# Constants packed so that the operands of the matrix products start at other offsets in a partition

## The chip, the cores and the metric

The kernel runs on one core of one Trainium2 chip. The metric is device time in microseconds (us), the median of three runs: 1645.25 us before the change (1645.24 to 1646.19). The engines are named as the profile names them: PE multiplies matrices (PEld is its loading of weights), DVE and ACT work elementwise, POOL is almost unused here, and SP issues nearly all transfers. SBUF, the memory on the core, has 128 partitions; a tile takes the same bytes of every partition, so its place is one number, its **offset** in a partition. This text is about those offsets.

## The reference, cut to what matters

A two-layer encoder over 512 tokens of 1024 features, all in float32. Each layer normalises, projects to 6144 columns, runs differential attention and a two-way gated recurrence (HGRN2) side by side, merges them under gates, and adds a SwiGLU feed-forward network of 2816 hidden features:

```python
for layer in range(DEPTH):
    h = rmsnorm(x, attn_norm[layer])
    proj = h @ w_in[layer]
    ...
    y_a = diff_attention(a_q, a_k, a_v, ...) @ w_a[layer]
    y_b = hgrn2_bidirectional(b_q, b_ff, b_fb, b_i, b_g, ...) @ w_b[layer]
    merged = jax.nn.sigmoid(gate_a) * y_a + jax.nn.sigmoid(gate_b) * y_b
    x = x + merged @ w_o[layer]
    h = rmsnorm(x, ffn_norm[layer])
    x = x + (jax.nn.silu(h @ w_gate[layer]) * (h @ w_up[layer])) @ w_down[layer]
return rmsnorm(x, final_norm)
```

## The kernel before

**Products in three parts.** Each float32 operand of a large product is split into a high part (rounded to the type that the code calls F32R) and a low part, the rest. `mm3` (L209 to L211) then issues three matmuls into one sum: high by high, high by low, low by high. One matmul has a *stationary* operand, 128x128, which PE loads first, and a *moving* one, 128 partitions by 512 columns of 4 bytes, which is 2048 bytes of each partition. In the profile `m<-hh,hi` is: output `m`, moving operand `hh`, stationary operand `hi`.

**Who moves and who stands.** `xT` is the residual, `hh` and `hl` are the two parts of the normed input: 8 chunks of 128 features by 512 tokens, so 2048 bytes a chunk. The weights come in by `wload` into two buffers `raw`, and `wsplit` makes `hi` (ACT, L92) and `lo` (DVE, L81) of them, three buffers each. `project_fm` and the feed-forward loop hold the weights still and move the activations (`hh`, `hl`, `mh`, `ml`, `obh`, `obl`, `oah`, `oal`, or `gh`, `gl`). `project_tm` and the last `w_down` hold the activations still (512 bytes of a chunk at a time) and move the weights.

**Stages of a layer.** Projections from `hh`, `hl` and the HGRN2 heads, four projections with tokens on partitions (`project_tm`), attention, `w_b` and `w_a`, `w_o` (moving `mh`, `ml`), then gate and up of the feed-forward network (moving `hh`, `hl`), then `w_down` (`gh`, `gl`: moving in the first layer, stationary in the second). Of the matmuls with 512 moving columns, 3648 move `hh` or `hl`, 768 have `hh` or `hl` stationary, and 2120 have neither.

**What sets the order.** A scheduler orders each engine's instructions by the order of the code, by priority (`urgent`) and by some orders written by hand (`behind`). It doesn't look at offsets.

**What sets the offsets.** Pools take SBUF in the order in which they are opened, and a tile takes its size rounded up to 32 bytes. The pool `const` comes first, behind 1152 bytes that the system keeps. In it `eps` and `one`, 4 bytes each, take 32 bytes each, and `rcol` and `rcol8`, 16 bytes each, stand behind `hh`, `hl` and `rbc`. Behind `const` come `wraw` (`raw`), `wsplit` (`hi`, `lo`), `small`, and then the pools that each stage opens.

Of the kernel before, what the change touches and what calls it, by code (L numbers as in the profile page):

```python
# [9 lines left out]
F32 = mybir.dt.float32  # L10
# [8 lines left out]
P = 128  # L19
# [12 lines left out]

# column offsets of the combined input projection
A_Q, A_K, A_V, B_Q, B_FF, B_FB, B_I, B_G, G_A, G_B = (
    0, 512, 1024, 1536, 2048, 2560, 3072, 3584, 4096, 5120)

# columns of the transposed small vectors
V_ATT, V_FFN, V_DA, V_HG, V_LB = 0, 16, 32, 40, 48


def _bits(x, n):
    """x cut to n significand bits."""
    m, e = math.frexp(x)
    return math.ldexp(math.floor(m * (1 << n)), e - n)
# [3 lines left out]
def kernel(  # L48
# [45 lines left out]
    def behind(ins, other):  # L94
        """Queue ins after other, on whatever engines they are."""
        tc.add_manual_dep(ins.ins, other.ins.name,
                          mybir.DependencyInfo(mybir.DependencyClass.NoSync, mybir.DependencyReason.DATA),
                          reason="keep the tensor engine from waiting")
# [13 lines left out]

    # ---------------------------------------------------------------- constants
    ident = cp.tile([P, P], F32, name="ident")
# [4 lines left out]
    DVE.tensor_copy(ones_r, ones)  # L119
    eps = cp.tile([P, 1], F32, name="eps")  # L120
    DVE.memset(eps, EPS)
    one = cp.tile([P, 1], F32, name="one")
    DVE.memset(one, 1.0)
# [3 lines left out]

    # block-diagonal masks of blocks of 2**j tokens, j = 0..4
    masks = cp.tile([P, 5, P], I8, name="masks")
# [8 lines left out]

    # ------------------------------------------------- residual and normed input
    xT = cp.tile([P, DC, T], F32, name="xT")  # L140
    hh = cp.tile([P, DC, T], F32R, tag="hh", name="hh")
    hl = cp.tile([P, DC, T], F32R, tag="hl", name="hl")
    rbc = cp.tile([P, T], F32, name="rbc")
    rcol = cp.tile([P, TC], F32, name="rcol")
    rcol8 = cp.tile([P, TC], F32, name="rcol8")
    sacc = cp.tile([P, T], F32, name="sacc")
# [3 lines left out]
    def normed(src, c, gain):  # L150
        """Chunk c of the normed input, up to the row scale, in two parts."""
        hi = act(hh[:, c, :], src, AF.Copy, scale=gain)
        return hi, stt(hl[:, c, :], src, gain, hh[:, c, :].bitcast(F32), ALU.mult, ALU.subtract)
# [9 lines left out]
    def absorb(c, gain, first):  # L163
        """Chunk c of the new residual."""
        normed(xT[:, c, :], c, gain)
        squares(c, first)
# [20 lines left out]

    # ------------------------------------------------------------ weight streams
    def wload(src):
        """src: [p, k, c] of DRAM."""  # L190
        _, k, c = src.shape
        raw = wp.tile([P, 2048], F32, tag="raw", name="raw")
        v = raw[:, :k * c].rearrange("p (k c) -> p k c", c=c)
        load(v, src)
        return v

    def wsplit(v):
        """hi and lo parts of v [p, k, c]."""
        _, k, c = v.shape
        hi = hp.tile([P, 1024], F32R, tag="hi", name="hi")[:, :k * c].rearrange("p (k c) -> p k c", c=c)  # L200
        lo = hp.tile([P, 1024], F32R, tag="lo", name="lo")[:, :k * c].rearrange("p (k c) -> p k c", c=c)
        split_act(v, hi, lo)
        return hi, lo
# [9 lines left out]
    def project_fm(w, cols, evac, k=DC, ah=None, al=None):  # L213
        """Output features on partitions; cols: list of first columns (128 wide), pairs adjacent."""
        ah = hh if ah is None else ah
# [21 lines left out]
    def project_tm(w, c0, evac):  # L237
        """512 output features from column c0, tokens on partitions."""
        ps = [mbank() for _ in range(TC)]
# [15 lines left out]

    # ------------------------------------------------------------------- start
    lnexp = ACT.preload_act_table_set("natural_log_exp_and_others")
# [8 lines left out]
    with tc.tile_pool(name="init", bufs=1, reuse_waits="tile") as ip:  # L266
# [41 lines left out]
        with tc.issue_after(norms[-1][1].ins):  # L308
            for c in range(DC):
                squares(c, c == 0)  # L310

            # differential weights [1, -lambda] of each layer
            lv = lam.rearrange("p (g j e) -> p g j e", j=2, e=64)
# [12 lines left out]

            # lower bounds of the second layer's forget gates, columns (direction, head)
            lg = vecs[:, V_LB:V_LB + 16].rearrange("p (d l h) -> p d l h", d=2, l=2)
# [17 lines left out]

            # rotary tables
            sins = []
# [36 lines left out]

    # ------------------------------------------------------------------- HGRN2
    def sigmoid(v):
        """In place, by exponentials and logarithms alone."""
        act(v, v, AF.Exp, scale=-1.0)
        act(v, v, AF.Ln, bias=one)  # L390
        return act(v, v, AF.Exp, scale=-1.0)
# [10 lines left out]
    def head_norm(ps, sq, sh, sl, gain, mark):  # L402
        """rmsnorm of ps [value, token] over its partitions, times gain."""
        ss = bank("hss")
        mm = PE.matmul(ss, ones_r, sh, start=True, stop=False)
        if mark is not None:
            behind(mm, mark)
        PE.matmul(ss, ones_r, sl, start=False, stop=True)
        rsqrt_mean(sq, ss, P)
        stt(sq, ps, gain, sq, ALU.mult, ALU.mult)  # L410
        return sq

    def hgrn_head(l, h, q, z, sg, vB, oh, ol, hgp):
        """q [P,T]; z [P,2,T] gate inputs (forward, backward); sg [P,T] output gate input;
        vB [P,TC,512]; oh, ol [P,T] result in two parts."""
        flat = lambda v: v.rearrange("p d c -> p (d c)")
        blocks = lambda v: v.rearrange("p (b c) -> p b c", c=64)
        # log forget gates g, with a zero before each 64 tokens, and log keys lk
        lk = hgp.tile([P, 2, T], F32, tag="lk", name="lk")
# [10 lines left out]
        else:  # L430
# [9 lines left out]
            tt(lk, lk, z, ALU.subtract)  # L440
        # products of each query with its own token's key and, times one decay, its neighbour's
        kk = z
# [7 lines left out]
        tt(kk, kk, q.unsqueeze(1).to_broadcast([P, 2, T]), ALU.mult)  # L450
        # sums within 64 tokens: cf, cb inclusive, xb exclusive; key exponents
        for d in range(2):
# [5 lines left out]
        tt(ab, ab, xb, ALU.add)  # L458
        # totals of 64 tokens; before and from each 64 within its chunk of 128; decays of whole chunks
        tot = cum[:, :, :, 64]  # L460
# [10 lines left out]
        def chunk_states(d):  # L471
            """Queries decayed from (to) the chunk's edge and the states they meet there."""
            f = hgp.tile([P, 2, T], F32, tag="fac", name="fs", bufs=FAC)
# [17 lines left out]
        def turned(f, kc):  # L491
            """The keys with their tokens on partitions."""
            pt = bank("kt")
# [23 lines left out]
        def level(L):  # L517
            """Decayed queries and keys of the blocks of 2 L tokens about their middles."""
            f = hgp.tile([P, 2, T], F32, tag="fac", name="fl", bufs=FAC)
# [22 lines left out]

        # transposed scores within chunks: rows s, columns t
        A = hgp.tile([P, TC, P], F32, tag="A", name="A")
# [9 lines left out]
        def place(L, pv):  # L554
            """The blocks of 2 L tokens of A."""
            if L == 64:
# [12 lines left out]
        kb, turn = turned(fb, bk)  # L569
        # the wide levels first; each narrower one takes its blocks over  # L570
        done = None
# [39 lines left out]

    # --------------------------------------------------------------- attention
    def rope(v, tp):
        """v [P, TC, 512], in place."""
        w = v.rearrange("p t (g e) -> p t g e", e=64)
# [11 lines left out]

    def attention(l, aq, ak, avh, avl, oh, ol, ap):
        """aq, ak (rotated, queries scaled) [P, TC, 512]; avh, avl the values in two parts;
        oh, ol [P, HEADS, T] result in two parts."""  # L630

        def operands(h):
            """Each component's two parts stacked on the partitions: queries, keys, keys the other way round."""
            half = [slice(0, 64), slice(64, 128)]
# [20 lines left out]
        def exps(q2, ka, kb, t, mark):  # L655
            """Exponentials of both components' scores of 128 queries, and their sums."""
            tok = slice(t * P, (t + 1) * P)
# [61 lines left out]

    # ------------------------------------------------------------------ layers  # L720
    last_silu = None
    for l in range(LAYERS):
        win = w_in[l]
        an = [vecs[:, V_FFN + 8 * l + c:V_FFN + 8 * l + c + 1] for c in range(DC)]
        with ExitStack() as mix:
# [10 lines left out]
            def scaled(dst):  # L736
                """dst(i): where tile i goes."""
                return lambda i, ps: tt(dst(i), ps, rbc, ALU.mult)
# [180 lines left out]
def _layout(inputs):  # L919
    """The input with its features first; the vectors that go with features as columns of 128."""  # L920
    import numpy as _np
# [27 lines left out]
```

## Time and profile before

| | |
|---|---|
| median of the runs | 1645.25 us |
| the profiled execution, first to last instruction | 1645.1 us |
| instructions | 18701 |
| DVE busy | 1011.9 us (62%) |
| ACT busy | 777.0 us (47%) |
| bytes moved | 142.53 MB, mean 87 GB/s |

The span of the profiled execution is 0.15 us under the median, so nearly nothing lies around it. Matmuls overlap one another: the profile gives one with 512 columns some 390 to 400 ns, but the next starts after some 230 ns. What a matmul costs in a dense row is therefore the distance from its start to the next start. It is read from the timeline, or from the number of matmuls in a stretch.

### The profile page before, as it was taken

How to read it: one execution, taken by the hardware profiler on the slowest of the kernel's cores; microseconds unless marked ns; L12 is line 12 of the kernel's file. 1: busy time of each engine (PE TensorE's matmuls, PEld its weight loads, DVE VectorE, ACT ScalarE, POOL GpSimd, SP SyncE). 2: the span in 40 equal slices, each digit the busy share in tenths (PEclk: the TensorE clock that was granted, in tenths of full speed). 3: DMA queues.
4: the chain of work that ended last, by engine and by line, in shares of the span. 5: the costliest groups of instructions: out<-in, count | busy, mean ns of one | idle time of the engine just before them, and what ended most of it. 6: DMA issues, size and time to landing. Idle time of an engine off the chain costs nothing.

```text
span 1645.1 us, 18701 instructions
## 1 busy us (share of the span) xinstructions
PE 1625.3 (99%) x7456; PEld 1325.9 (81%) x7456; DVE 1011.9 (62%) x1626; ACT 777.0 (47%) x1192; POOL 7.8 (0%) x21
## 2 busy tenths in 40 slices
PE   8999999999999999999999999999999999999998
PEld 6788888887888888888878888888878888888886
DVE  7878977877644444433368789688875444444224
ACT  5666666676432322322255567676744323224213
POOL 1000000000000000000000000000000000000000
PEclk9999999999999999999999999999999999999999
DMA  5312212221332223322232222122123233322321
GB/s 186 96 58 77 77 52 77 77 77 51 103 102 85 92 79 102 103 90 97 97 101 77 77 77 75 56 76 77 51 78 103 77 103 103 103 94 98 103 79 75
DMA packets 118823, 142.53 MB, mean 87 GB/s; under 512 B 3024, under 2 KB 101328, under 8 KB 118736
## 3 DMA queue, kind: packets, MB, share of 16 engines
q1 hardware_dynamic: 118592, 141.31, 26.1%
q8 instruction: 58, 0.95, 0.2%
q14 instruction: 29, 0.24, 0.0%
q10 hardware_dynamic: 144, 0.03, 0.0%
HBM read 139.23 MB, written 2.10 MB: 86 GB/s over the span
## 4 chain that ended last, share of the span: by engine, by line
PE 94%; DVE 3%; ACT 2%; issue 1%; DMA 0%; SPq 0%; ACTq 0%
PE m L211 27%; PE m L209 27%; PE m L210 27%; PE sc L550 2%; DVE fl L81 1%; PE po L600 1%; PE s L209 1%; PE s L210 1%; PE s L211 1%; PE qk L666 1%; PE wt L713 1%; PE qk L663 1%; PE st L503 1%; ACT fl L78 0%; DVE lo L81 0%
## 5 line engine op out<-in xcount | busy, mean ns | idle before, releaser
L92 ACT CAST hi<-raw 128x1024 fp32r<-128x1024 f32 (+2 forms) x280 | 276.5, 989 | 631.3 <-PE m L210 486.6
L209 PE MATMUL m<-hh,hi 128*128 128x512 f32 x1216 | 483.7, 398 | 7.2 <-ACT hh L78 7.2
L210 PE MATMUL m<-hl,hi 128*128 128x512 f32 x1216 | 483.4, 398 | 0.1
L211 PE MATMUL m<-hh,lo 128*128 128x512 f32 x1216 | 483.4, 398 | 0.0
L81 DVE TENSOR_TENSOR lo<-raw,hi 128x1024 fp32r<-128x1024 f32 (+2 forms) x280 | 320.7, 1146 | 183.6 <-ACT hi L92 182.1
L209 PEld LDWEIGHTS m<-hh,hi 128*128 128x128 f32 x1216 | 229.6, 189 | 61.0 <-ACT hh L78 7.9
L210 PEld LDWEIGHTS m<-hl,hi 128*128 128x128 f32 x1216 | 229.5, 189 | 54.8 <-DVE hl L84 1.4
L211 PEld LDWEIGHTS m<-hh,lo 128*128 128x128 f32 x1216 | 229.4, 189 | 53.2
L81 DVE TENSOR_TENSOR gu<-m,rbc 128x512 f32<-128x512 f32 x88 | 60.9, 692 | 255.1 <-PE m L211 251.1
L209 PE MATMUL m<-hi,hh 128*128 128x512 f32 x256 | 102.2, 399 | 0.0
L211 PE MATMUL m<-hi,hl 128*128 128x512 f32 x256 | 101.7, 397 | 0.0
L210 PE MATMUL m<-lo,hh 128*128 128x512 f32 x256 | 101.7, 397 | 0.0
L78 ACT ACTIVATE fl<-fl 128x1024 f32<-128x1024 f32 (+1 forms) x56 | 48.4, 872 | 42.7 <-DVE fl L81 42.6
L210 PE MATMUL m<-gl,hi 128*128 128x512 f32 x176 | 68.6, 390 | 0.0
L211 PE MATMUL m<-gh,lo 128*128 128x512 f32 x176 | 68.6, 390 | 0.0
L209 PE MATMUL m<-gh,hi 128*128 128x512 f32 x176 | 68.6, 389 | 0.0
L211 PEld LDWEIGHTS m<-hi,hl 128*128 128x128 f32 x256 | 48.3, 189 | 9.9
L210 PEld LDWEIGHTS m<-lo,hh 128*128 128x128 f32 x256 | 48.3, 189 | 9.9
L209 PEld LDWEIGHTS m<-hi,hh 128*128 128x128 f32 x256 | 48.3, 189 | 9.8
L550 PEld LDWEIGHTS sc<-fl 128*128 128x128 f32 x384 | 49.1, 191 | 6.5 <-DVE fl L81 2.7
L550 PE MATMUL sc<-fl 128*128 128x128 f32 x384 | 51.2, 277 | 1.2 <-DVE fl L81 1.2
L210 PE MATMUL m<-ml,hi 128*128 128x512 f32 x128 | 49.8, 392 | 0.0
(254 smaller groups left out, 2337.5 us busy)
## 6 DMA issues: line engine op xcount, KB each, us to landing
raw<-in_w_in_dram SPq DMA_DIRECT2D x47, 1024.0 KB, 5.2
raw<-in_w_gate_dram SPq DMA_DIRECT2D x22, 1024.0 KB, 5.2
raw<-in_w_up_dram SPq DMA_DIRECT2D x22, 1024.0 KB, 5.2
raw<-in_w_down_dram SPq DMA_DIRECT2D x19, 1024.0 KB, 5.0
raw<-in_w_o_dram SPq DMA_DIRECT2D x8, 1024.0 KB, 5.2
raw<-in_w_b_dram SPq DMA_DIRECT2D x4, 1024.0 KB, 4.9
raw<-in_w_a_dram SPq DMA_DIRECT2D x4, 1024.0 KB, 4.9
raw<-in_w_down_dram SPq DMA_DIRECT2D x4, 768.0 KB, 4.3
```

Of the source, the lines that this page charges most:

```text
L78: return ACT.activation(o, i, func, **kw)
L81: return DVE.tensor_tensor(o, a, b, op)
L92: return ACT.copy(hi, src), tt(lo, src, hi.bitcast(F32), ALU.subtract)
L209: PE.matmul(ps, lh, rh, start=start, stop=False)
L210: PE.matmul(ps, lh, rl, start=False, stop=False)
L211: PE.matmul(ps, ll, rh, start=False, stop=stop)
L503: mm = PE.matmul(ps[:, i * P:(i + 1) * P], kt[:, i, :], vB[:, kc + i, h * P:(h + 1) * P], start=True, stop=True)
L550: mm = PE.matmul(ps[:, c], K[:, c], Q[:, c], start=True, stop=True)
L600: mm = PE.matmul(po[:, tok], a, b, start=i == 0, stop=i == len(terms) - 1)
L663: mm = PE.matmul(ps[c], q2[:, c, tok], ka[:, c, :], start=True, stop=False)
L666: PE.matmul(ps[c], q2[:, c, tok], kb[:, c, :], start=False, stop=True)
L713: tr = PE.transpose(pt[:, s * P:(s + 1) * P], w[:, 0, s * P:(s + 1) * P], ident)
```

## The change

`eps` and `one` become two columns of one tile `fixed`, which takes 32 bytes in the place of 64; `rcol` and `rcol8`, 32 bytes each, move from behind `rbc` to ahead of `xT`. Comments and docstrings are taken out, and from there on a line of code stands one line later.

```diff
-    eps = cp.tile([P, 1], F32, name="eps")
+    fixed = cp.tile([P, 2], F32, name="fixed")
+    eps, one = fixed[:, 0:1], fixed[:, 1:2]
     DVE.memset(eps, EPS)
-    one = cp.tile([P, 1], F32, name="one")
     DVE.memset(one, 1.0)
...
+    rcol = cp.tile([P, TC], F32, name="rcol")
+    rcol8 = cp.tile([P, TC], F32, name="rcol8")
     xT = cp.tile([P, DC, T], F32, name="xT")
     hh = cp.tile([P, DC, T], F32R, tag="hh", name="hh")
     hl = cp.tile([P, DC, T], F32R, tag="hl", name="hl")
     rbc = cp.tile([P, T], F32, name="rbc")
-    rcol = cp.tile([P, TC], F32, name="rcol")
-    rcol8 = cp.tile([P, TC], F32, name="rcol8")
     sacc = cp.tile([P, T], F32, name="sacc")
```

No instruction is added, removed, made larger or moved: every engine's row is the same in the same order, on all five engines, but for the tile `fixed` that stands where `eps` or `one` did. What differs is where the tiles lie. The offsets as the build places them, in bytes:

| tile | before | past 2 KiB | past 128 | after | past 2 KiB | past 128 |
|---|---|---|---|---|---|---|
| `ident` | 1152 | 1152 | 0 | 1152 | 1152 | 0 |
| `xT` | 6112 | 2016 | 96 | 6144 | 0 | 0 |
| `hh` | 22496 | 2016 | 96 | 22528 | 0 | 0 |
| `hl` | 38880 | 2016 | 96 | 38912 | 0 | 0 |
| `raw`, first buffer | 59424 | 32 | 32 | 59392 | 0 | 0 |
| `hi`, first buffer | 75808 | 32 | 32 | 75776 | 0 | 0 |
| `lo`, first buffer | 88096 | 32 | 32 | 88064 | 0 | 0 |
| `mh` | 191008 | 544 | 32 | 190976 | 512 | 0 |
| `gh`, `obh` (different times) | 109088 | 544 | 32 | 109056 | 512 | 0 |
| `fl`, `fs` (HGRN2), first buffer | 203424 | 672 | 32 | 203392 | 640 | 0 |

"Past 2 KiB" is the remainder by 2048, "past 128" by 128. The further chunks and buffers of a tile are whole multiples of 512 bytes on, so the last column holds for all slices that PE reads. So before the change `hh` and `hl` start 32 bytes ahead of a multiple of 128 (and of 2048), and all other operands of PE, but for the constants `ident` and `ones_r`, 32 bytes behind a multiple of 128 (outside the HGRN2 heads also of 512); after it, all operands of PE start at a multiple of 128. `xT`, `hh`, `hl` and `rbc` move up by 32 bytes, and all that follows moves down by 32.

## The prediction

> **What bounds the kernel now.** The page comes first: the share of each engine and the chain of work that ended last.
>
> ```profile
> PE 1625.3 (99%) x7456; PEld 1325.9 (81%) x7456; DVE 1011.9 (62%) x1626; ACT 777.0 (47%) x1192; POOL 7.8 (0%) x21
> ...
> PE 94%; DVE 3%; ACT 2%; issue 1%; DMA 0%; SPq 0%; ACTq 0%
> PE m L211 27%; PE m L209 27%; PE m L210 27%; PE sc L550 2%; DVE fl L81 1%; PE po L600 1%; PE s L209 1%; PE s L210 1%; PE s L211 1%; PE qk L666 1%; PE wt L713 1%; PE qk L663 1%; PE st L503 1%; ACT fl L78 0%; DVE lo L81 0%
> ```
>
> PE is 94% of the chain, four fifths of the span are the three matmul lines of `mm3`, and no transfer is on the chain. PE sits idle for 1645.1 - 1625.3 = 19.8 us in all. So only the pace of the matmuls can move the time by much. The groups of instructions show that the pace isn't one number:
>
> ```profile
> L209 PE MATMUL m<-hh,hi 128*128 128x512 f32 x1216 | 483.7, 398 | 7.2 <-ACT hh L78 7.2
> ...
> L209 PE MATMUL m<-hi,hh 128*128 128x512 f32 x256 | 102.2, 399 | 0.0
> ...
> L209 PE MATMUL m<-gh,hi 128*128 128x512 f32 x176 | 68.6, 389 | 0.0
> ...
> L210 PE MATMUL m<-ml,hi 128*128 128x512 f32 x128 | 49.8, 392 | 0.0
> ```
>
> Same shape, same type, no idle time ahead of nearly all of them, and yet 398 and 399 ns wherever `hh` takes part against 389 and 392 ns with `gh` or `ml`. These durations overlap, so I count matmuls in stretches of one kind each (PE busy and in brackets the matmuls, then PEld, DVE and ACT; behind POOL the granted clock). In order: `hh`, `hl` moving in the feed-forward network; `gh`, `gl` moving; `mh`, `ml` moving; `hh`, `hl` stationary; `gh`, `gl` stationary.
>
> ```profile
> 480.00:680.00 200.00, 200.00 (x859) 161.47 (x858) 90.14 (x108) 58.32 (x72) 0.00 (x0) 1.00 0.29 95
> 720.00:820.00 100.00, 100.00 (x443) 82.80 (x442) 34.53 (x39) 27.12 (x34) 0.00 (x0) 1.00 0.29 98
> 415.00:455.00 40.00, 40.00 (x177) 32.85 (x176) 25.07 (x33) 16.00 (x22) 0.00 (x0) 1.00 0.29 93
> 859.00:879.00 20.00, 20.00 (x88) 16.21 (x87) 19.93 (x34) 13.13 (x22) 0.00 (x0) 1.00 0.17 55
> ...
> 1530.00:1630.00 100.00, 100.00 (x442) 82.55 (x441) 26.34 (x26) 21.36 (x27) 0.00 (x0) 1.00 0.22 76
> ```
>
> A matmul counts if it touches the stretch, so the distance between starts is (length + one duration) / count: (200 + 0.40) / 859 = **233.3 ns** for `hh` moving, (100 + 0.39) / 443 = **226.6 ns** for `gh`, 40.39 / 177 = 228.2 ns for `mh`, 20.40 / 88 = 231.8 ns for `hh` stationary, 100.39 / 442 = 227.1 ns for `gh` stationary. PE is busy all of the time and the clock is 1.00 in each, so neither waits nor the clock make the difference. The timeline shows the step itself, from `hh` to `gh`, with no pause in it:
>
> ```profile
> 701.84 0.39 PE L209 MATMUL m<-hh,hi 128*128 128x512 f32 x1
> ...
> 703.00 0.40 PE L211 MATMUL m<-hh,lo 128*128 128x512 f32 x1
> 703.24 0.40 PE L209 MATMUL m<-gh,hi 128*128 128x512 f32 x1
> ...
> 703.94 0.39 PE L209 MATMUL m<-gh,hi 128*128 128x512 f32 x1
> ...
> 708.02 0.39 PE L209 MATMUL m<-gh,hi 128*128 128x512 f32 x1
> ```
>
> Six matmuls from 701.84 to 703.24 are 0.2333 us each, eighteen from 703.94 to 708.02 are 0.2267 us each; three at the joint still run slow. What else differs? Line, shape, PSUM tile and weight buffers are the same; `w_o` even runs through the same `project_fm` with the same 8 chunks. More DVE and ACT work isn't it: `mh`, with DVE busy for 25.07 of 40 us (63%), is faster than `hh` with 45%. What is left is the data, and the place: `hh` and `hl` start 96 bytes past a multiple of 128, `gh`, `gl`, `mh`, `ml` and the weights 32 past. I read the 6.7 ns as the price of that place.
>
> **The change part by part.**
>
> *`hh` and `hl` moving, 3648 matmuls.* They come to a multiple of 2048, and `hi`, `lo` as well. No row shows a matmul of 512 columns whose operands both start at a multiple of 128, so the new pace is bounded. From above: it loses the 6.7 ns that the nearest row, `gh`, doesn't pay, or, were a common start as bad as the present one is against `gh`, pays them twice (240.0 ns). From below: the far end is the weight load. Each matmul follows the load that begins when the one before it starts:
>
> ```profile
> 800.05 0.19 PEld L211 LDWEIGHTS m<-gh,lo 128*128 128x128 f32 x1
> 800.27 0.39 PE L211 MATMUL m<-gh,lo 128*128 128x512 f32 x1
> ```
>
> so 190 ns, which for all 6536 matmuls would be some 250 us less. The nearer bound are matmuls of 128 columns with the moving operand in either place: `fs`, `A` (32 past a multiple of 128) and the transposes, which move `ident` (at a multiple already).
>
> ```profile
> 145.13 0.39 PE L600 MATMUL po<-A,vB 128*128 128x128 f32 x2
> ...
> 145.80 0.39 PE L600 MATMUL po<-A,vB 128*128 128x128 f32 x2
> ...
> 260.24 0.60 PE L639 MATMUL qkt<-ident,aq 128*128 128x128 f32 x4
> 260.67 0.60 PE L639 MATMUL qkt<-ident,ak 128*128 128x128 f32 x4
> ```
>
> Six take 0.67 us, 111.7 ns each; four transposes take 0.43 us, 107.5 ns each: 3.8% less, but a transpose is another kind of matmul. By that ratio 226.6 would become 218.0 ns. I take 226.6 ns, the row of the same instruction and the nearest in place: 3648 x 6.7 ns = **24.4 us** less, of which 2112 x 6.7 = 14.2 us in the feed-forward network and 10.3 us in the mixing stages.
>
> *`hh` and `hl` stationary, 768 matmuls.* From 231.8 to 227.1 ns, the row with `gh` stationary: 768 x 4.7 = **3.6 us** less.
>
> *The other 2120 matmuls of 512 columns*, and those of 128: from 32 past to a multiple. Between +6.7 and -8.6 ns each by the same bounds (+14 to -18 us in all); I take nothing, since both ends are guesses about a place that no row shows.
>
> *DVE and ACT.* Their operands move as well. For DVE two rows stand on either side of the present difference, `xT` 96 past and `gb` 32 past a multiple of 128:
>
> ```profile
> L81 DVE TENSOR_TENSOR xT<-xT,m 128x512 f32<-128x512 f32 x24 | 16.5, 689 | 41.4 <-PE m L211 41.4
> ...
> L81 DVE TENSOR_TENSOR gb<-gb,m 128x512 f32<-128x512 f32 x16 | 11.0, 685 | 0.4
> ```
>
> 4 ns in 689, on an engine that is 3% of the chain: 0.6% of 1011.9 us is 6 us of busy time, 0.2 us on the chain. Nothing, either way. ACT, 2% of the chain, I bound by the same share.
>
> *Transfers.* 0% of the chain; a weight block takes 5.2 us to land, and is loaded ahead:
>
> ```profile
> raw<-in_w_gate_dram SPq DMA_DIRECT2D x22, 1024.0 KB, 5.2
> ```
>
> Eight chunks by three matmuls by two column blocks are 48 matmuls, 11.2 us of PE work for each block of 1024 KB. The cover stays if PE is 3% faster, and were it gone, the rest of a landing would show as waits of PE for `raw`, which it doesn't have now. The moves of `rcol`, `fixed` and so on cost nothing: the same instructions on the same few columns.
>
> *What is late next.* In the feed-forward network DVE is at 90.14 of 200 us, far from binding. In the mixing stages it is not: 19.93 of 20 us in the stretch 859 to 879, though PE doesn't wait there. Of the 10.3 + 3.6 = 13.9 us that fall into these stages I give back 2 us to chains of DVE and ACT that don't get faster.
>
> Sum: 24.4 + 3.6 - 2.0 = 26.0 us. The profiled execution, 1645.1 us, becomes 1619.1, and with 0.15 us around it to the median of 1645.25 us, **1619.2 us**.
>
> **The rivals.**
>
> *It goes further.* At a multiple of 128 the moving read also loses what 32 past may cost now. For it: 96, 32 and 0 past would be a row from bad to good, and the transposes are at its end. Against: it rests on matmuls of another kind. At 218.0 ns throughout: 3648 x 15.3 + 768 x 13.8 + 2120 x 8.6 = 84.6 us less, 1561 us; with what DVE would then hold back, anything from 1548 to 1612.
> [...]
>
> *Nothing changes*: the pace doesn't hang on where a tile starts, and the change doesn't do what it says. For it: the pace has a memory. At the joint to `project_tm` the weights become the moving operand, and the pace stays at (862.84 - 857.71) / 22 = 0.2332 us:
>
> ```profile
> 857.71 0.40 PE L209 MATMUL m<-hi,hh 128*128 128x512 f32 x1
> ...
> 862.84 0.40 PE L210 MATMUL m<-lo,hh 128*128 128x512 f32 x1
> ```
>
> It may be a beat between weight loads and matmuls that `hh` falls into by its data or by lying low in the partition (22 to 55 KB, `gh` from 109). Against: 1056 matmuls a layer stay in it, and `gh` leaves it within three. The time would be 1645.2 us.
> [...]
>
> *Slower*: a common start collides. `hh` and the weights then start at the same remainder by 2048, where they now lie 64 bytes apart, and PE reads both at once. If equal remainders are what costs, a matmul goes to 240.0 ns as bounded above: 3648 x 6.7 = 24.4 us more, 1669.7 us; it decides if the feed-forward stretch shows over 233.3 ns. Against: `gh` and `hi` start at equal remainders by 512 today, and are the fastest.
>
> *Given back*: the gain of the mixing stages, 13.9 us, is lost to DVE, and the feed-forward network's 14.2 us remain: 1631 us. Against: PE idles for 19.8 us in all.
>
> **How the numbers follow.** The forecast (1612 to 1626) has 0.48, further (1548 to 1612) 0.28 and beyond it 0.02, given back (1626 to 1636) 0.05, nothing 0.12, slower 0.05. The predicted time is the likeliest, 1619.2. The range from 1548 to 1630 holds 0.48, 0.28 and most of the 0.05, together 0.8. It is wide on the low side since no row shows an aligned pair. About 0.2%, 3.3 us, is what a measurement can tell from no change. Faster by more: 0.48 + 0.28 + 0.02 + 0.05 = 0.83; within it 0.12; slower 0.05.
>
> **What would show it.** In the feed-forward stretch, 200 us would hold (200 + 0.39) / 0.2266 = 884 matmuls for 859, and `m<-hh,hi` would come to 390 ns from 398; in `project_tm` the pace would be 227 ns; in the stretches of `gh` and `mh` the counts stay at 443 and 177. If the `gh` stretch holds 460 or more, it goes further; if `hh` keeps 859, place isn't the cause; fewer than 859 is the collision. More idle time of PE than 19.8 us, behind DVE in the mixing stages, is the gain given back. The forecast is wrong if the 6.7 ns belong to the data or to a beat that alignment doesn't break.

## The result, and the profile after

The changed kernel takes **1628.11 us** (median of 4 runs, 1627.93 to 1628.52), beside 1645.72 us for the kernel before in the same comparison (4 runs, 1645.24 to 1646.24). The ratio is 0.9893, with a 95% interval from 0.9879 to 0.9907: 17.6 us, 1.1% faster. The forecast was 1619.2 us, so the sign and the stretch were right and a third of the gain didn't come. The profiled execution spans 1626.2 us, 18.9 us less than before.

The page of after: busy time of the engines, and the chain that ended last by engine and by line.

```profile
PE 1604.3 (99%) x7456; PEld 1323.7 (81%) x7456; DVE 1010.8 (62%) x1626; ACT 776.6 (48%) x1192; POOL 7.8 (0%) x21
...
PE 85%; DVE 9%; ACT 4%; issue 1%; DMA 0%; SPq 0%; ACTq 0%
PE m L210 24%; PE m L212 24%; PE m L211 24%; DVE fl L81 2%; DVE lo L81 2%; PE sc L551 2%; PE s L212 1%; PE s L211 1%; PE s L210 1%; PE qk L667 1%; DVE z L81 1%; PE wt L714 1%; PE po L601 1%; PE qk L664 1%; ACT hi L92 1%
```

The counts of instructions are the same, PE is busy for 21.0 us less, DVE and ACT for as long as before. The chain now runs over DVE for 9% instead of 3%, and PE idles for 1626.2 - 1604.3 = 21.9 us instead of 19.8. The groups (mean ns of one behind the busy time) show which matmuls got shorter:

```profile
L210 PE MATMUL m<-hh,hi 128*128 128x512 f32 x1216 | 476.7, 392 | 7.1 <-ACT hh L78 7.1
...
L210 PE MATMUL m<-hi,hh 128*128 128x512 f32 x256 | 101.5, 396 | 0.0
...
L210 PE MATMUL m<-gh,hi 128*128 128x512 f32 x176 | 68.5, 389 | 0.0
...
L211 PE MATMUL m<-ml,hi 128*128 128x512 f32 x128 | 49.7, 391 | 0.0
```

Where `hh` takes part, 398 and 399 ns became 392 and 396; `gh` stays at 389, and `ml` goes from 392 to 391. The five stretches in the order of the prediction, each moved to where the same stage now lies (the stretch of stationary `hh` is 18 us). A count can be off by one matmul, which is 0.3 ns of the pace in 200 us, but 2.6 ns in 20 us:

```profile
470.00:670.00 200.00, 200.00 (x884) 165.60 (x883) 92.60 (x110) 60.56 (x74) 0.00 (x0) 1.00 0.30 95
700.00:800.00 100.00, 100.00 (x443) 82.81 (x442) 33.74 (x37) 26.35 (x32) 0.00 (x0) 1.00 0.30 98
410.00:450.00 40.00, 40.00 (x178) 32.78 (x176) 25.67 (x35) 16.54 (x23) 0.00 (x0) 1.00 0.32 106
850.00:868.00 18.00, 18.00 (x81) 14.91 (x80) 17.96 (x32) 11.40 (x20) 0.00 (x0) 1.00 0.19 62
1510.00:1610.00 100.00, 100.00 (x442) 82.46 (x441) 25.55 (x25) 21.71 (x26) 0.00 (x0) 1.00 0.23 80
```

In the feed-forward network 200 us hold 884 matmuls instead of 859: (200 + 0.39) / 884 = 226.7 ns for 233.3. `gh` moving stays at 443, `mh` at 178 (177 before), `gh` stationary at 442; the clock is 1.00 throughout, as before. At the joint from `hh` to `gh` the timeline has no step any more:

```profile
692.68 0.39 PE L211 MATMUL m<-hl,hi 128*128 128x512 f32 x1
...
694.49 0.39 PE L210 MATMUL m<-gh,hi 128*128 128x512 f32 x1
...
701.06 0.39 PE L212 MATMUL m<-gh,lo 128*128 128x512 f32 x1
```

Eight matmuls take 1.81 us up to the joint and twenty-nine take 6.57 us behind it: 0.2263 and 0.2266 us each.

By stages, from the starts of matmuls in both traces: gate and up of the feed-forward network go from 247.04 to 240.19 us in the first layer and from 249.59 to 242.70 in the second, **13.7 us** together. `w_o` and `w_down` change by 0.03 us at most. The mixing stages go from 406.73 to 404.86 us and from 400.44 to 397.21, **5.1 us** together. That is where the forecast had 11.9. The 5.1 is good to some 1.5 us: in the first layer these stages take 406.73 us before the change and 405.29 with the constants alone, 404.86 after it and 403.39 with the two small tiles alone (both kernels come below), at the same paces.

### The profile page after: what moved, and what is told of

The parts are those of the page before. It is cut to its first block, busy times and chain, and to the rows that moved or that the text cites. A ratio compares the mean times of both kernels' runs of the same rounds, so it can differ in the third digit from the quotient of the medians.

```text
span 1626.2 us, 18701 instructions
## 1 busy us (share of the span) xinstructions
PE 1604.3 (99%) x7456; PEld 1323.7 (81%) x7456; DVE 1010.8 (62%) x1626; ACT 776.6 (48%) x1192; POOL 7.8 (0%) x21
## 4 chain that ended last, share of the span: by engine, by line
PE 85%; DVE 9%; ACT 4%; issue 1%; DMA 0%; SPq 0%; ACTq 0%
PE m L210 24%; PE m L212 24%; PE m L211 24%; DVE fl L81 2%; DVE lo L81 2%; PE sc L551 2%; PE s L212 1%; PE s L211 1%; PE s L210 1%; PE qk L667 1%; DVE z L81 1%; PE wt L714 1%; PE po L601 1%; PE qk L664 1%; ACT hi L92 1%
## 5 line engine op out<-in xcount | busy, mean ns | idle before, releaser
L210 PE MATMUL m<-hh,hi 128*128 128x512 f32 x1216 | 476.7, 392 | 7.1 <-ACT hh L78 7.1
L211 PE MATMUL m<-hl,hi 128*128 128x512 f32 x1216 | 476.1, 392 | 0.1
L212 PE MATMUL m<-hh,lo 128*128 128x512 f32 x1216 | 476.2, 392 | 0.0
L210 PEld LDWEIGHTS m<-hh,hi 128*128 128x128 f32 x1216 | 229.2, 188 | 54.6 <-ACT hh L78 7.9
L211 PEld LDWEIGHTS m<-hl,hi 128*128 128x128 f32 x1216 | 228.9, 188 | 48.0 <-DVE hl L84 1.4
```

The costliest lines, as they stand in the source:

```text
L210: PE.matmul(ps, lh, rh, start=start, stop=False)
L211: PE.matmul(ps, lh, rl, start=False, stop=False)
L212: PE.matmul(ps, ll, rh, start=False, stop=stop)
```

## The experiments

The prediction put the price on a place, 96 bytes past a multiple of 128. Two questions were left over: why 0 past should be no better than 32 past, and why `gh` with the same weights was fast already. A second theory answers both. What counts is the **distance** of the moving from the stationary operand, as a remainder by some number: the offset of `hh` less that of the weights. By 256, `hh` lay 64 below the weights before (224 and 32), and `gh` lay at 0. The first four kernels tell the two theories apart; the later ones look for the period, for the pair of reads that pays, and for the gain that mixing lost. Each ratio is to the kernel before; the stretch quoted is the 200 us in the feed-forward network, where PE never waits.

### Half the change: constants only

The kernel before, with `eps` and `one` in one tile, and `rcol`, `rcol8` where they were. `hh` and the weights both move down by 32 bytes: places 64 and 0 past 128, the distance still -64.

```diff
-    eps = cp.tile([P, 1], F32, name="eps")
+    fixed = cp.tile([P, 2], F32, name="fixed")
+    eps, one = fixed[:, 0:1], fixed[:, 1:2]
...
-    one = cp.tile([P, 1], F32, name="one")
```

> Only eps and one are packed: hh, hl start 64 past a multiple of 128, the weights and all later pools at a multiple of 128. Theory 'own place' (a moving operand 96 past is slow, 0 and 32 past are fast): hh is no longer at 96, so most or all of the 6.7 ns goes if 64 past counts as good, and the feed-forward stretch of 200 us holds some 884 matmuls for 859; time near 1628 us. Rival 'distance' (the pace is set by how far the moving and the stationary operand lie apart): hh and the weights lie 64 apart as before the change, so 859 matmuls, 233.3 ns and 1645 us, same as before. Matmuls that move gh or mh keep 226.6 to 228.2 ns by either.

```profile
470.00:670.00 200.00, 200.00 (x859) 160.29 (x858) 89.11 (x108) 58.38 (x72) 0.00 (x0) 1.00 0.30 95
```

1645.5 us, ratio 1.0 (0.999 to 1.0009), and 859 matmuls as before. With the weights at a multiple of 2048 and `hh` at another place than before, nothing changed.

### Half the change: the two small tiles only

The kernel before, with `rcol` and `rcol8` ahead of `xT`. `hh` and the weights both lie 32 past a multiple of 128: the distance is 0, and nothing is aligned to 128.

```diff
+    rcol = cp.tile([P, TC], F32, name="rcol")
+    rcol8 = cp.tile([P, TC], F32, name="rcol8")
     xT = cp.tile([P, DC, T], F32, name="xT")
...
-    rcol = cp.tile([P, TC], F32, name="rcol")
-    rcol8 = cp.tile([P, TC], F32, name="rcol8")
```

> Only rcol and rcol8 move: hh, hl and the weights all start 32 past a multiple of 128 (and of 2048 at their first chunk), no large operand at a multiple. Both theories, own place and distance: 227 ns for hh, 884 matmuls in 200 us of the feed-forward network, time as after the change, 1628 us. Rival 'multiples of 2 KiB are what counts': 859 matmuls and 1645 us, or a pace between.

```profile
470.00:670.00 200.00, 200.00 (x884) 165.65 (x883) 92.61 (x110) 60.59 (x74) 0.00 (x0) 1.00 0.31 95
```

1627.39 us, ratio 0.9888 (0.9873 to 0.9903): the whole gain, from this half alone. The multiples of 2 KiB add nothing: the changed kernel, which has them, holds 884 as well.

### A pad behind the constants, and the same pad ahead of them

Both are the changed kernel with 96 unused bytes. Behind `sacc` they leave `hh` at 0 and move all later pools to 96 past 128: distance -96, and `gh` with its weights 96 past, 0 apart. Ahead of `xT` they put everything 96 past, the place on which the prediction laid the price, at distance 0.

```diff
     sacc = cp.tile([P, T], F32, name="sacc")
+    cp.tile([P, 24], F32, name="pad")
```

> The changed kernel with 96 unused bytes behind sacc: hh, hl stay at a multiple of 128, the weights and all later pools come to 96 past. Own place: matmuls that move hh stay at 227 ns, those that move gh, mh or the weights go to 233 ns (528 + 528 + 384 + 768 of them and more, 2888 x 6.5 ns = some 15 to 19 us), time near 1645 us. Distance: hh and the weights are 96 apart, so hh goes to 233 ns or more (3648 x 6.5 = 24 us), while gh and mh lie 0 apart from the weights and stay at 227 ns; time near 1645 us too, but the stretches tell: feed-forward 884 and w_down 430 by own place, 859 and 443 by distance.

```diff
+    cp.tile([P, 24], F32, name="pad")
     xT = cp.tile([P, DC, T], F32, name="xT")
```

> The changed kernel with 96 unused bytes ahead of xT: every large operand is 96 past a multiple of 128, and any two of them are 0 apart. Own place: all 6536 matmuls of 512 columns go to 233 ns, 6536 x 6.5 ns = some 42 us over the changed kernel less what waits hide, near 1665 us; slower than before. Distance: all stay at 227 ns, 1628 us.

The pad behind, `hh` and then the stretch of `gh` moving:

```profile
470.00:670.00 200.00, 200.00 (x855) 160.82 (x854) 89.08 (x106) 57.70 (x71) 0.00 (x0) 1.00 0.30 92
710.00:810.00 100.00, 100.00 (x443) 82.84 (x442) 33.73 (x37) 26.14 (x32) 0.00 (x0) 1.00 0.30 98
```

The pad ahead:

```profile
470.00:670.00 200.00, 200.00 (x884) 165.65 (x883) 92.61 (x110) 60.58 (x74) 0.00 (x0) 1.00 0.31 95
```

1649.76 us, ratio 1.0022 (1.0013 to 1.0031), against 1627.84, ratio 0.989 (0.9874 to 0.9907). The first has `hh` and `hl` at multiples of 2 KiB and is as slow as the kernel before, a little slower. The second has them 96 past 128 and is as fast as the changed kernel. In the first `gh` is 96 past as well and holds 443. The place falls as a cause; the distance holds.

### Other distances

The pad behind `sacc` with 32, 128 and 256 bytes, `[P, 8]`, `[P, 32]` and `[P, 64]` in the line above.

> The changed kernel with 32 unused bytes behind sacc: the weights and later pools start 32 past a multiple of 128, hh and hl at a multiple; distance 32. So far distance 0 gave 227 ns, 64 gave 233.3, 96 gave 234.1. If the price grows with the distance: between 227 and 233 ns, some 230 ns, 870 matmuls in 200 us of the feed-forward network, time near 1637 us. If any distance within 128 costs the same: 233 ns, 859 and 1645 us. gh and mh stay at 227 ns.

> The changed kernel with 128 unused bytes behind sacc: distance 128 between hh and the weights. If distances count by their remainder by 128: as the changed kernel, 227 ns, 884 matmuls, 1628 us. If they count by 256 or 512: 233 ns or more, 859 or fewer, 1645 us or more.

> The changed kernel with 256 unused bytes behind sacc: hh and the weights are 256 apart. Distances 32, 64, 96 and 128 gave 232.5 to 234.1 ns, 0 (and whole multiples of 512, as between the chunks) 227. If distances count by their remainder by 256: 227 ns, 884 matmuls in 200 us of the feed-forward network, 1628 us. If by 512: 859 or fewer, 1645 us or more.

In that order, one row from each trace:

```profile
470.00:670.00 200.00, 200.00 (x859) 161.04 (x858) 89.17 (x107) 57.95 (x72) 0.00 (x0) 1.00 0.30 94
```

```profile
470.00:670.00 200.00, 200.00 (x859) 160.93 (x858) 89.20 (x106) 58.11 (x72) 0.00 (x0) 1.00 0.30 93
```

```profile
470.00:670.00 200.00, 200.00 (x884) 165.62 (x883) 92.60 (x110) 60.56 (x74) 0.00 (x0) 1.00 0.30 95
```

1647.27 us (1.0007, from 0.9997 to 1.0017), 1644.83 us (0.999, from 0.998 to 0.9999) and 1628.08 us (0.9889, from 0.9874 to 0.9903). So 128 bytes isn't a period, and 256 is one as far as 0 and 256 show: these give 226.7 ns, while 32, 64 and 128 (the weights above) give 233.3, and 96 gives 200.39 / 855 = 234.4. By the starts in these stretches, single distances are even where the remainders are equal (226 and 227 ns). Where they aren't, most spread: from 231 to 235 ns at 32, 230 to 237 at 64 before the change, 230 to 238 at 96 and 229 to 238 at 128. With the constants alone, at 64 as well, they are 233 and 234: the mean is the same, the spread isn't.

### Only the low weights apart

The changed kernel with 64 bytes between the first `hi` and `lo`: `hh`, `hl` and `hi` stay at 0, `lo` and the later pools lie 64 past. Does a matmul pay for the distance to its own weights, or for that to the weights that are loaded while it runs, those of the next one?

```diff
+                wh = hp.tile([P, 1024], F32R, tag="hi", name="hi")
+                if i == 0:
+                    hp.tile([P, 16], F32, tag="pad", name="pad", bufs=1)
+                wl = hp.tile([P, 1024], F32R, tag="lo", name="lo")
...
```

> The changed kernel with 64 unused bytes between hi and lo: hh, hl and hi start at a multiple of 512, lo and all later pools 64 past one. The matmuls come in threes: (hh, hi), (hl, hi), (hh, lo), and while one runs the weights of the next are loaded. Theory 'next load' (the moving read and the load of the next weights, which run at the same time, get in each other's way unless they start at the same remainder by 512): the distance from (hl, hi) to its next start is long, 233 ns or more, those from (hh, hi) and (hh, lo) stay at 227; in w_down, where gh lies 64 past, (gh, hi) and (gh, lo) are long and (gl, hi) is short. Rival 'own weights': (hh, lo) is long and the other two short; in w_down (gh, hi) and (gl, hi) long, (gh, lo) short. Time between 1628 and 1645 us by both.

The stretch in the feed-forward network and that of the first `w_down`, then the groups of three stages (from 480 to 680 us, 720 to 810 and 1535 to 1630), the busiest first:

```profile
470.00:670.00 200.00, 200.00 (x867) 162.57 (x866) 90.97 (x109) 58.97 (x72) 0.00 (x0) 1.00 0.30 95
710.00:810.00 100.00, 100.00 (x438) 82.05 (x438) 33.48 (x37) 26.16 (x32) 0.00 (x0) 1.00 0.29 95
```

```profile
L212 PE MATMUL m<-hh,lo 128*128 128x512 f32 x289 | 114.9, 397 | 0.0
L211 PE MATMUL m<-hl,hi 128*128 128x512 f32 x289 | 113.3, 392 | 0.0
L210 PE MATMUL m<-hh,hi 128*128 128x512 f32 x289 | 112.4, 389 | 0.0
...
L210 PE MATMUL m<-gh,hi 128*128 128x512 f32 x132 | 51.9, 393 | 0.0
L212 PE MATMUL m<-gh,lo 128*128 128x512 f32 x132 | 51.5, 390 | 0.0
L211 PE MATMUL m<-gl,hi 128*128 128x512 f32 x131 | 51.2, 391 | 0.0
...
L211 PE MATMUL m<-lo,gh 128*128 128x512 f32 x72 | 28.8, 400 | 0.0
L210 PE MATMUL m<-hi,gh 128*128 128x512 f32 x72 | 28.5, 398 | 0.0
L212 PE MATMUL m<-hi,gl 128*128 128x512 f32 x72 | 28.2, 392 | 0.0
```

In the feed-forward network the one that pays most is `m<-hh,lo`, which runs with its own weights 64 away while weights at distance 0 are loaded: by the starts it takes 235.8 ns to the next one, `m<-hh,hi` 228.3 and `m<-hl,hi` 229.2. The theory of the next load, as it stands, falls there. `w_down` of the first layer, where `gh` now lies 64 above `hi`, goes from 226.6 to (100 + 0.39) / 438 = 229.2 ns, less than 64 below costs. In the last `w_down`, however, `m<-lo,gh` takes the longest, 237.8 ns, with both operands 64 past and so 0 apart, and neither theory says that.

One reading, made afterwards from the same trace, fits the order in all three stages: compare the weights of a matmul with what the matmul *before* it moves, since they are loaded while that one runs (in the changed kernel a load of 0.19 us for `m<-hh,lo` begins at 560.08 us, where `m<-hl,hi` starts, and `m<-hh,lo` starts at 560.30). It is the theory of the next load with the price seen one matmul later; a matmul is on record for 389 to 400 ns and the next starts after some 225 to 240, so neighbours overlap, and a start doesn't say when the reading begins. By this count 64 apart are `m<-hh,lo` (235.8 ns, beside 228.3 and 229.2); `m<-gh,hi` and `m<-gl,hi` of the first `w_down` (230.4 and 228.9, beside 227.6); `m<-hi,gh` and `m<-lo,gh` of the last one (235.5 and 237.8, beside 229.9). In `project_tm` single distances swing from 224 to 241 ns and settle nothing. No run was made to test this reading, and why a sign counts stays open. No run moves the tiles of DVE, ACT or the transfers alone, but the price depends on which of the three matmuls it is, and that speaks against their reads and writes as the other side. The time is 1646.04 us, ratio 0.9999 (0.9989 to 1.0008): 64 bytes at one pair of weight tiles and the later pools give back the whole gain.

### Where mixing loses its gain: shorter chains

Of the 13.9 us that the forecast saw in mixing, 5.1 came. Is that the chains of DVE and ACT in the HGRN2 heads, which don't get faster? Both kernels with these chains shortened: the levels 16, 8, 4 and 2 take the queries and keys of level 32 and don't build their own, so that part of the recurrence's arithmetic is left out; PE has the same matmuls (7456 on each page).

```diff
-            *kq, mark = level(L)
+            if L >= 32:
+                *kq, mark = level(L)
```

> The kernel before, leaving out part of the HGRN2 heads: the decayed queries and keys of the levels 16, 8, 4 and 2 are not computed, their score matmuls read those of level 32; PE has the same 7136 matmuls, DVE and ACT have some 76 and 34 us less in the mixing stages. Theory 'given back to chains': PE of the kernel before hardly waited for these chains, so it gets only a little faster, by 2 to 10 us.

> The changed kernel with the same part left out. Given back to chains of DVE and ACT: with the chains shortened the gain against short_before comes nearer to the 28 us that the paces alone give, 21 to 27 us, in place of the 17.6 measured between the full kernels. Rival 'restarts' (after each pause or group of small matmuls PE runs at 230 to 236 ns for a while, whatever the offsets): the gain stays at 17 to 19 us.

1649.16 us (ratio to the kernel before 1.0017, from 1.0008 to 1.0026) and 1628.35 us (0.9889, from 0.9875 to 0.9904). With DVE busy for 952.2 us instead of 1011.9, the kernel before should have become 2 to 10 us faster and did not. The changed kernel didn't get faster either (1628.11 us with the full chains). What this says of the chains is limited, since the rest didn't stay as it was: in the mixing stages of the kernel before, the part of long distances between starts that lies over 240 ns fell from 24.7 to 21.1 us, but the small matmuls `sc`, `nr` and `po` took some 4.9 us more from start to start.

The gain between the two is 20.8 us by the medians, where the full kernels have 17.6. The spans of the profiled executions give 19.2 (1645.3 and 1626.1), but the former belongs to the fastest of ten runs (1647.35 us; the others took 1648.52 and more). Mixing saves 5.2 us in these two executions, beside 5.1. That lies between the two theories; the length of the chains isn't shown to be the cause.

## Why the prediction was right, and where it was not

**That only the pace of the matmuls counts, and that the change moves it: right.** PE is still 99% busy, and of the 18.9 us that the span lost, 18.84 lie in the stages that use `hh` and `hl`.

**"I read the 6.7 ns as the price of that place": wrong, and harmless by luck.** The pad ahead of `xT` has the place and not the price (226.7 ns); the pad behind `sacc` has the price and not the place (234.4 ns). With `hh` moving in the feed-forward network, 226.7 ns goes with remainders by 256 that are equal for `hh`, `hl` and all their weights, and 233.3 to 234.4 ns with `hh` and `hl` at another remainder than the weights. The change took `hh` off its place and brought it to distance 0 in one step, so the wrong cause gave the right pace: the row taken for it, `gh`, has `gh` and `hi` at equal remainders (32 and 32).

**The feed-forward term: right.** 884 matmuls were forecast for the 200 us and 884 are there, and 13.7 of 14.2 us came.

**The other 2120 matmuls at nothing: right**, with a reason that the prediction lacked: they were at distance 0 before and are after, but for 72 with the constant `ones_r`. For the same reason "it goes further" fell: going from 32 to 0 past 128 with both operands leaves the distance at 0. The count of `gh` stays at 443, not 460. Nor does any run show a pace that would give the low end of the range, 1548 us: the fastest stretch of 100 us or more holds 443 matmuls in 100 us, 226.6 ns each.

**"A common start collides": the reverse.** Equal remainders gave 226.7 ns, unequal ones 233.3 to 234.4. The prediction had the row for it, "`gh` and `hi` start at equal remainders by 512 today, and are the fastest", and used it as an objection only; read as the cause, it would have named the distance, up to its period.

**"Nothing changes"** fell for the whole change and for the second half of it, but is exact for the first half: the constants alone give 1.0.

**The mixing stages: mis-sized.** "I give back 2 us" left 11.9 us, and 5.1 came. The table goes by the starts in both traces. A distance counts for a pace if another matmul of 512 columns follows within 245 ns; of the longer ones the part over 240 ns counts as pause.

| | forecast | measured |
|---|---|---|
| `hh`, `hl` moving | 1536 x 6.7 ns = 10.3 us | 233.2 to 228.0 ns over some 1412 distances = 7.3 us |
| `hh`, `hl` stationary | 768 x 4.7 ns = 3.6 us | 230.7 to 228.3 ns over 698 distances = 1.7 us |
| longer pauses | -2.0 us | 24.7 to 28.0 us = -3.3 us |
| remainder, small matmuls | 0 | -0.6 us |

So 4.9 us of the miss lie in the pace, for two reasons. The stretch 859 to 879, read as 231.8 ns from a count of 88, stood for all 768 with `hh` stationary. By the starts it runs at 233.3 ns, and other `project_tm` stretches of the kernel before (from 240 us and from 1056 us) at 228.9, at the same distance; hence the mean of 230.7. What sets these two paces, no run shows.

And the matmuls between other work come to 228.0 and 228.3 ns after the change, not to the 226.6 of a row that nothing interrupts. Both traces say where that is lost. Count the matmuls with `hh` or `hl` in the mixing stages from the last interruption, which is a pause over 245 ns or a matmul of another kind:

| | first 6 | 7 to 12 | 13 to 24 | from the 25th |
|---|---|---|---|---|
| before | 232.1 ns | 232.1 ns | 232.6 ns | 232.7 ns |
| after | 230.7 ns | 227.8 ns | 227.2 ns | 226.7 ns |

After the change, what lies over 226.7 ns adds up to 3.4 us, and all but 0.01 us of it falls on the first 24 matmuls behind an interruption. So it is the restarts, as the rival of the last experiment had it; whether a pause or the other matmul makes them slow, the count doesn't separate.

The other 1.9 us lie in pauses and small matmuls. How a pause grows is seen where PE waits for ACT. Two rows of the view of PE's waits (total us, times, longest us), before and after:

```profile
PE sc L550 <- DVE fl L81: 1.2, 3, 0.7
PE st L503 <- ACT kt L498: 0.8, 1, 0.8
```

```profile
PE st L504 <- ACT kt L499: 2.0, 1, 2.0
...
PE sc L551 <- DVE fl L81: 1.5, 3, 1.0
```

And the longest of these in the two timelines, before and after:

```profile
80.44 0.40 PE L211 MATMUL m<-hi,hl 128*128 128x512 f32 x1
81.67 1.49 PE L503 MATMUL st<-vB,kt 128*128 128x128 f32 x11 [0.84 <-ACT kt L498]
```

```profile
78.95 0.40 PE L212 MATMUL m<-hi,hl 128*128 128x512 f32 x1
81.31 1.60 PE L504 MATMUL st<-vB,kt 128*128 128x128 f32 x12 [1.96 <-ACT kt L499]
```

PE's last matmul ahead of the wait starts 80.44 - 78.95 = 1.49 us earlier, and what waits for `kt` starts 81.67 - 81.31 = 0.36 us earlier: 1.13 us of a gain are lost at one place. This one repeats: the wait is 1.96 us in the traces of all four kernels with equal remainders (after, the two small tiles alone, the pad ahead, the pad of 256), and 0.78 to 0.99 us in those of the five in which `hh` and the weights are unequal throughout.

**"Given back", 1631 us**: partly what happened, and given too little. 1628.11 us lies in the band from 1626 to 1636 us, which had a chance of 0.05, and not in the forecast's own, from 1612 to 1626; the whole range ends 1.9 us above it. Mixing kept 5.1 of its 13.9 us, not none, and more was lost to the pace there than to waits for DVE and ACT.

**"With 0.15 us around it": too little.** It set the median beside the span of another execution. The runs on record with their own spans have 1.7 to 2.2 us around them; the median after is 1628.11 - 1626.2 = 1.9 us over the profiled span. The profiled execution before, 1645.1 us, must then have taken some 1646.8 us or more, over all four runs behind the median of 1645.72; so the spans differ by 18.9 us and the medians by 17.6. The miss of 8.9 us is then 6.8 in mixing, 0.4 in the feed-forward network and 1.75 here.

**DVE, ACT and transfers at nothing: right.** 1010.8 and 776.6 us busy, and DMA is 0% of the chain.

## What to carry to other kernels

In a dense row of matmuls with 512 columns of 4 bytes, give all moving operands and all weights the same remainder by 256 bytes: here that was 226.7 ns in place of 233.3 to 234.4. Whether it was 0, 32 or 96 made no difference (884 matmuls in 200 us each), and one moved pair of 32-byte tiles was worth the whole gain. When two groups of equal instructions run at different paces, compare every pair of operands, not each operand alone. And the pace of a row that nothing interrupts isn't reached at once where other work comes between: here the first six matmuls behind an interruption took 230.7 ns each, those from the 25th on 226.7. Count those apart. Read a pace from the starts, too, where the stretch is short.

## What the runs showed of the hardware

With the same instructions in the same order, the time from start to start of a matmul of 512 columns is 226.7 ns where the two operands start at equal remainders by 256, and 233.3 to 234.4 ns at 32, 64, 96 and 128 (weights above); the clock is 1.00 in all of these. That holds for `hh` moving in the feed-forward network, with `hi` and `lo` at one remainder; with `hh` stationary, before the change, the pace was 233.3 ns in some stretches and 228.9 in others.

The load of the next weights runs beside a matmul: in the changed kernel one load takes 0.188 us on average for `m<-hh,lo`, and the one at 560.08 us begins as the matmul before starts. The paces differ by 3% with nothing but offsets of tiles changed. That the read of the moving operand and the read of that load get in each other's way is the author's reading; it fits the order of paces with the low weights apart (235.8 ns beside 228.3 and 229.2 in the feed-forward network), but no run was made to show it.
